# One key and one value piece per step in a cached attention's decode, TensorE's order written out there, and the start of the second group's decode moved

## The chip, the cores and the metric

The kernel runs on one core of one Trainium2 chip. A core has TensorE (PE, matmuls and transposes), VectorE (DVE), ScalarE (ACT), GpSimd (POOL) and SyncE (SP, which here only issues DMAs), each with its own queue of instructions. The time is that of one execution on the device in microseconds, lower is better; the median of several runs is given.

## What is computed

One layer of an encoder on a prompt of 1024 tokens and, beside it, on 8 sequences of 16 new tokens that have a cache of past keys and values. The heads fall in two groups of 8: group A does stick-breaking attention over the full past, group B attention over a band with a learned bias.

```
h = rmsnorm(x, g_mix)
q_a, k_a, v_a, q_b, k_b, v_b = split_heads(h, w_in)
# prompt:  a   = stick_breaking(q_a, k_a, v_a)          o_b = chunk_band_prompt(q_b, k_b, v_b, rel_table)
# decode:  a   = stick_breaking(q_a, [past_sb_k, k_a], [past_sb_v, v_a])      past of 1024
#          o_b = band_attention(q_b, [past_cb_k, k_b], [past_cb_v, v_b])      past of 512
x = x + concat(rmsnorm(a), rmsnorm(o_b)) @ w_out
h = rmsnorm(x, g_ffn)
x = x + (silu(h @ w_gate) * (h @ w_up)) @ w_down
x = x + sigmoid(rmsnorm(x, g_ple) @ w_ple_gate) * (p @ w_ple_proj)

def stick_breaking(q, k, v):
    z = einsum('bqhd,bkhd->bhqk', q, k) * HEAD_DIM ** -0.5
    log_keep = where(causal, log_sigmoid(-z), 0)
    between = cumsum(log_keep, reverse) - log_keep
    w = where(causal, exp(log_sigmoid(z) + between), 0)
    return einsum('bhqk,bkhd->bqhd', w, v)
```

The new keys and values are outputs too.

## The kernel before

Tokens are rows: 8 tiles of 128 prompt tokens and one tile of 128 decode tokens (8 sequences x 16), so 9 tiles or 3 token groups of 384. Every f32 operand of the projections is split in a high and a low part, and a product is three matmuls (`mm3`, L105 to L107); the low part of weights, `wlo`, is made by POOL, and the helper that makes it has one line, L110.

The part of the program that matters here has four stages. First the hidden state is normed and transposed into `hT` (two halves of the rows, three token groups, high and low). Then `project` (the generator `qkv`) runs over twelve chunks of 256 columns of `w_in`, (group, q/k/v, chunk); `queries` and `others` yield after each piece of about 24 matmuls. 36 of its yields run by themselves. In the next 30, A's decode runs beside it: `advance(project, dec, 2.2, 30)` calls the decode 2.2 times for each yield of the projection. Then A's attention (`att`) runs beside the rest of the projection, the last chunk of which is (1, 0, 1), B's second query chunk; after it the pools of the projection close. Last, B's decode and the product with `w_ple_proj` (`embed`, whose sums are named pj) run beside the rest of attention: six yields of the decode to one of attention's stages, then `along(dec, embed(), 0.55)` at 1.3 for each.

The decode works on sequences n (a batch, 16 tokens x 8 heads = 128 rows) and chunks c of 256 cached tokens; 4 chunks for A, 2 for B. Its list `seq` alternates a key piece and a value piece, the value pieces some places behind. `fetch` loads a piece of 512 KB into a buffer `draw` (7 buffers in A, 6 ahead; in B one less) over SP's queue, L134. `prepare` of a key piece makes eight transposes (L383) and copies them to `kT`; that of a value piece transposes two or three tiles of weights `wdec` and `wn` (L392, in `flip`). `scores` are four matmuls into rows of 32 of `sdec` (L406), and on the last chunk one with the causal mask (L409); `outputs` are four per tile of values, into `acc` (L449). A matmul of f32 leaves two records in the trace, a bf16 one. When a batch has all its scores, `weights` makes the scan over keys and the multiply on DVE (L424, L425) and `wn` on POOL (L437). A step of the decode handles one piece: fetch six ahead, prepare two ahead, then scores or outputs.

In attention S are the scores (L551), `w` the weights, whose last product is made by POOL (L566, tiles of 128x127 to 128x1023), then transposed on PE (L584) and split by ACT and DVE, and po are the outputs (L607, L608). In B's decode POOL also scales `bias` (L327) and adds the two parts of new values, queries and keys, `nv`, `sq`, `sk` (L341, L334).

The order on each engine comes from Tile's scheduler, which simulates a timeline of all engines and puts each engine's instructions in the order that it finds. A block under `tc.manual_schedule(engines={...})` keeps, on the engines named, the order in which the code issues. Buffers of a pool are laid over those of closed pools, and an instruction that writes one waits until the last reader of the old contents is done.

Of the kernel before, what the change touches and what calls it, by code (L numbers as in the profile page):

```python
# [22 lines left out]
P = 128  # L23
# [9 lines left out]
SKEW = 2  # L33
LAG, RAWS, PT = 5, 7, 2
# [4 lines left out]
def tile_hymba_step(  # L39
# [119 lines left out]
    class Transposed:  # L159
# [5 lines left out]
        def add(self, pool, half, name):  # L165
            for n in range(2):
                for g in range(3):
                    self.t[n][g][half] = pool.tile([P, KT // 2, 384], F32R, name=f"{name}{'hl'[n]}{g}{half}")
# [47 lines left out]
    def qkv(ch, hT, stg):  # L216
# [16 lines left out]
        def queries(grp, c, wts):  # L233
            wh, wl = wts
            for pr in range(2):
                m = slice(pr * P, (pr + 1) * P)
                for g in range(3):
                    ps_ = ps["o"].tile([P, 384], F32, name="ps", tag="O")
                    for k in range(KT):
                        mm3(ps_, wh[:, k, m], wl[:, k, m], *hT.rows(g, k), k == 0, k == KT - 1)  # L240
                    transposed_out(grp, 0, c * 2 + pr, g, parts(384, ps_, (1 - 2 * grp) * HD**-0.5))
                    yield

        def others(grp, w, c, wts, gs):

            wh, wl = wts
            for g in gs:
                st = stg.tile([P, 3, 256], F32, name="st", tag="st", bufs=2)
                for o in range(3):
                    ps_ = ps["o"].tile([P, 256], F32, name="ps", tag="O")  # L250
                    for k in range(KT):
                        mm3(ps_, *hT.tok(g * 3 + o, k), wh[:, k], wl[:, k], k == 0, k == KT - 1)
                    (V.tensor_copy if o % 2 else A.copy)(st[:, o], ps_)
                    if o < 2:
                        yield
# [29 lines left out]
                yield  # L285
# [28 lines left out]
    def decode(grp, ch, dk):  # L314

        odd = dk.tile([P, 2], F32, name="odd")
        nc.sync.dma_start(odd, consts[:, 0:2])
        nkc = (4, 2)[grp]
# [29 lines left out]

        ks = [("k", n, c) for n in range(8) for c in range(nkc)]
        vs = [None] * (nkc + VLAG[grp]) + [("v", n, c) for n in range(8) for c in range(nkc)]  # L350
        seq = [x for pieces in zip_longest(ks, vs) for x in pieces if x]
        raws, split = {}, {}

        def fetch(i):
            kind, n, c = seq[i]
            src = ((cache_sb_k, cache_cb_k) if kind == "k" else (cache_sb_v, cache_cb_v))[grp]
            src = src[0, n, c * 256 : (c + 1) * 256]
            raws[i] = ch.raw(src.rearrange("(n p) h d -> p n (h d)", p=P), 2, 512)
# [38 lines left out]
        def scores(st, c, kT):  # L397
# [9 lines left out]
            if grp == 0:  # L407
                if masked:
                    T.matmul(sc[:, 256:], lhsT=identb, rhs=causalb, start=False, stop=True)  # L409
# [317 lines left out]
    hT.add(hp, 0, "hT")  # L727
    hT.add(hp, 1, "hT")
# [18 lines left out]
    advance(project, dec, 2.2, 30)  # L747
    for _ in dec:
        pass
# [65 lines left out]
    advance(att, dec, 0, 6)  # L815
    beside = along(dec, embed(), 0.55)
    advance(att, beside, 1.3, 40)
# [658 lines left out]
```

## Time and profile before

| what | value |
|---|---|
| median of 3 runs | 1763.65 us (1763.17 to 1764.24) |
| the profiled execution | 1761.44 us |
| its span in the trace | 1759.7 us |
| mean granted TensorE clock | 0.985 |
| PE, DVE, POOL, ACT busy | 1688.2, 1051.2, 804.7, 761.6 us |
| share of PE in the chain that ended last | 86% |

In the trace of the profiled execution, A's decode lies between about 139 and 325 us, the rest of the projection, beside attention, to about 527, B's decode and `embed` from there to about 700. The page of the profile has one number of busy time for each engine; a window does the same for a stretch, with the granted clock (1.00 is full) and the share of time for which the DMA engines were busy. In a timeline each row is one instruction or a run of like ones (x8), with its start, its duration and in brackets the idle time of the engine before it and who ended it. The end of a matmul is modelled, so the pace is read from the starts.

### The profile page before, as it was taken

To read this page: it belongs to the slowest core of one execution; us is meant where nothing else is said; L and a number is where in the kernel's file an instruction comes from. 1 tells how busy PE (TensorE), PEld (TensorE's weight loads), DVE (VectorE), ACT (ScalarE), POOL (GpSimd) and SP (SyncE) were. 2 spreads that over 40 slices of the span, in tenths; PEclk is the share of its full clock that TensorE was granted. 3 is DMA by queue.
4 is the path that set the end of the run, shared out by engine and by line. 5 is a ranking of instruction groups with operands and counts; after the bars stand their busy time and mean duration, and the time that the engine had idled before them with its cause. 6 is when DMAs were issued, how large, how long until landed. Compare 5 with 4: busy or idle time off the path is not lost.

```text
span 1759.7 us, 29028 instructions
## 1 busy us (share of the span) xinstructions
PE 1688.2 (96%) x11048; PEld 1469.3 (84%) x11048; DVE 1051.2 (60%) x1638; ACT 761.6 (43%) x1646; POOL 804.7 (46%) x635
## 2 busy tenths in 40 slices
PE   7999999999996899899989999999999999999998
PEld 7998888889995687787868888888888788887998
DVE  5212444257778566653686666666666598878635
ACT  5213434367766567743553333333233333333532
POOL 3214321277559322312345555555555465558354
PEclk9999999999998899999999999999999999999999
DMA  6756887656468696855422222222222684411123
GB/s 210 252 187 201 292 270 267 187 159 171 137 173 232 199 264 196 222 169 187 163 83 90 93 93 93 93 93 92 95 93 93 235 327 138 138 51 60 48 80 138
DMA packets 183467, 279.93 MB, mean 159 GB/s; under 512 B 15264, under 2 KB 115232, under 8 KB 181920
## 3 DMA queue, kind: packets, MB, share of 16 engines
q1 hardware_dynamic: 183328, 278.07, 49.4%
q8 instruction: 88, 1.44, 0.3%
q14 instruction: 51, 0.42, 0.1%
HBM read 198.47 MB, written 79.56 MB: 158 GB/s over the span
## 4 chain that ended last, share of the span: by engine, by line
PE 86%; DMA 4%; DVE 4%; POOL 3%; ACT 2%; issue 1%; SPq 0%; POOLq 0%; ACTq 0%; DVEq 0%
PE ps L998 19%; PE ps L105 9%; PE ps L106 9%; PE ps L107 8%; PE pt L1249 6%; PE ps L1249 4%; PE pt L998 3%; PE pt L584 3%; PE pt L383 2%; PE acc L449 2%; PE po L608 2%; PE po L607 2%; PE S L551 2%; PE sdec L406 1%; DMA v<-sv 1%
## 5 line engine op out<-in xcount | busy, mean ns | idle before, releaser
L110 POOL TENSOR_TENSOR wlo<-wraw,whi 128x512 fp32r<-128x512 f32 (+1 forms) x128 | 232.7, 1846 | 233.1 <-ACT whi L149 228.8
L105 PE MATMUL ps<-whi,hTh 128*128 128x256 f32 x576 | 168.9, 293 | 1.0 <-ACT sq L222 0.6
L106 PE MATMUL ps<-wlo,hTh 128*128 128x256 f32 x576 | 165.9, 288 | 1.0 <-POOL wlo L110 1.0
L107 PE MATMUL ps<-whi,hTl 128*128 128x256 f32 x576 | 166.6, 289 | 0.0
L149 ACT CAST whi<-wraw 128x512 fp32r<-128x512 f32 (+1 forms) x132 | 90.4, 749 | 98.0 <-PE ps L998 65.7
L565 DVE TENSOR_TENSOR_SCAN keep<-keep,zero 128x128 f32<-128x128 f32 (+4 forms) x64 | 100.9, 1585 | 38.5 <-ACT keep L557 37.8
L566 POOL TENSOR_TENSOR w<-w,keep 128x127 f32<-128x127 f32 (+4 forms) x64 | 89.2, 1405 | 66.4 <-DVE keep L565 57.9
L105 PEld LDWEIGHTS ps<-whi,hTh 128*128 128x128 f32 x576 | 110.9, 193 | 7.2 <-issue 5.0
L110 DVE TENSOR_TENSOR wtl<-pt,wth 128x512 fp32r<-128x512 f32 (+1 forms) x192 | 94.7, 514 | 32.0 <-ACT wth L588 31.1
L106 PEld LDWEIGHTS ps<-wlo,hTh 128*128 128x128 f32 x576 | 110.9, 192 | 3.2 <-issue 1.8
L107 PEld LDWEIGHTS ps<-whi,hTl 128*128 128x128 f32 x576 | 111.0, 193 | 0.3 <-issue 0.2
L584 PE MATMUL pt<-ident,w 128*128 128x128 f32 x528 | 92.0, 286 | 17.2 <-POOL w L566 13.5
L588 ACT CAST wth<-pt 128x512 fp32r<-128x512 f32 (+1 forms) x192 | 84.4, 464 | 37.8 <-PE pt L584 37.4
L584 PEld LDWEIGHTS pt<-ident,w 128*128 128x128 f32 x528 | 64.4, 146 | 27.1 <-POOL w L566 14.3
L105 PE MATMUL ps<-whi,hVh 128*128 128x256 f32 x288 | 81.8, 284 | 0.5 <-ACT hVh L1396 0.5
L106 PE MATMUL ps<-wlo,hVh 128*128 128x256 f32 x288 | 81.7, 284 | 0.0
L607 PE MATMUL po<-wth,vk 128*128 128x256 f32 (+1 forms) x304 | 80.7, 294 | 1.0 <-DVE wtl L110 1.0
L107 PE MATMUL ps<-whi,hVl 128*128 128x256 f32 x288 | 81.5, 284 | 0.0
L551 PE MATMUL S<-qk 128*128 128x384 f32 (+2 forms) x192 | 73.5, 385 | 4.7 <-DVE mxp L560 1.7
L608 PE MATMUL po<-wtl,vk 128*128 128x256 f32 (+1 forms) x304 | 77.0, 294 | 0.0
L384 DVE COPY kT<-pt 128x512 f32<-128x512 f32 x48 | 32.9, 688 | 65.9 <-PE pt L383 59.7
L110 POOL TENSOR_TENSOR actl<-actr,acth 128x1024 fp32r<-128x1024 f32 (+1 forms) x22 | 56.5, 2571 | 33.9 <-DMA sr<-acts 18.2
(351 smaller groups left out, 5402.6 us busy)
## 6 DMA issues: line engine op xcount, KB each, us to landing
draw<-in_cache_sb_k SPq DMA_DIRECT2D x32, 512.0 KB
draw<-in_cache_sb_v SPq DMA_DIRECT2D x32, 512.0 KB
act<-sg SPq DMA_DIRECT2D x11, 1152.0 KB
actr<-act SPq DMA_DIRECT2D x22, 576.0 KB
wraw<-in_w_in SPq DMA_DIRECT2D x12, 1024.0 KB
wraw<-in_w_gate SPq DMA_DIRECT2D x11, 1024.0 KB
wraw<-in_w_up SPq DMA_DIRECT2D x11, 1024.0 KB
v<-sv SPq DMA_DIRECT2D x36, 256.0 KB
```

The costliest lines, as they stand in the source:

```text
L105: T.matmul(out, lhsT=ah, rhs=bh, start=start, stop=False)
L106: T.matmul(out, lhsT=ah, rhs=bl, start=False, stop=False)
L107: T.matmul(out, lhsT=al, rhs=bh, start=False, stop=stop)
L110: eng.tensor_tensor(out, a, hi.bitcast(F32), op=ALU.subtract)
L149: A.copy(h[:, o], v[:, o])
L551: T.matmul(sc, lhsT=hd["qq"][:, qs], rhs=hd["kkh"][:, kc], start=True, stop=False)
L565: V.tensor_tensor_scan(rev, rev, zero[:, 0:1].to_broadcast([P, n]), 1.0, op0=ALU.mult, op1=ALU.add)
L584: T.transpose(pt[:, (c - c0) * P : (c - c0 + 1) * P], w[:, c * P : (c + 1) * P], ident)
L607: T.matmul(dst, lhsT=vs, rhs=wth[:, kb - base, c0:c1], start=(i == 0), stop=False)
L608: T.matmul(dst, lhsT=vs, rhs=wtl[:, kb - base, c0:c1], start=False, stop=(i == nkb - 1))
L998: T.matmul(out, lhsT=a[x][:, k], rhs=b[y][:, k], start=(not more and k == 0 and n == 0), stop=(k == 3 and n == 2), skip_group_check=more)
L1249: T.matmul(out, lhsT=a[i][:, x, m * P : (m + 1) * P], rhs=b[j][:, x], start=(not more and x == 0 and n == 0), stop=(x == 1 and n == 2), sk ...
```

## The change

`hT` is allocated token group by token group. The last query chunk, (1, 1) in `queries`, runs by token groups: both pairs of heads of group 0, then of group 1, then of group 2. `others` yields after each tile of tokens. The decode issues its first loads ahead of its constants; a step handles a key piece and a value piece together, prepares the next step's pieces, makes the scores and outputs of its own, then weights and finish. A's decode advances 1.2 steps for each yield of the projection, and PE's order there is that of the code. The mask is four matmuls of 32 columns. B's decode is called three times at its start instead of six, then 1.0 to `embed` and 1.0 to attention.

```diff
--- before.py
+++ after.py
+R2 = 1.2
...
-        def add(self, pool, half, name):
-            for n in range(2):
-                for g in range(3):
+        def add(self, pool, half, name, gs=range(3)):
+            for g in gs:
+                for n in range(2):
...
         def queries(grp, c, wts):
             wh, wl = wts
-            for pr in range(2):
+            order = [(pr, g) for pr in range(2) for g in range(3)]
+            if (grp, c) == (1, 1):
+                order.sort(key=lambda x: x[1])
+            for pr, g in order:
                 m = slice(pr * P, (pr + 1) * P)
-                for g in range(3):
...
         def others(grp, w, c, wts, gs):
...
                     (V.tensor_copy if o % 2 else A.copy)(st[:, o], ps_)
-                    if o < 2:
-                        yield
+                    yield
...
-                yield
...
     def decode(grp, ch, dk):
+        nkc = (4, 2)[grp]
+        ks = [("k", n, c) for n in range(8) for c in range(nkc)]
+        vs = [None] * (nkc + VLAG[grp]) + [("v", n, c) for n in range(8) for c in range(nkc)]
+        seq = [x for pieces in zip_longest(ks, vs) for x in pieces if x]
...
+        ahead = ch.raws - 1
+        for i in range(ahead):
+            fetch(i)
         odd = dk.tile([P, 2], F32, name="odd")
         nc.sync.dma_start(odd, consts[:, 0:2])
...
                 if masked:
-                    T.matmul(sc[:, 256:], lhsT=identb, rhs=causalb, start=False, stop=True)
+                    for pr in range(4):
+                        o = slice(pr * 32, pr * 32 + 32)
+                        T.matmul(sc[o, 256:], lhsT=identb[:, o], rhs=causalb, start=False, stop=True)
...
-        ahead = ch.raws - 1
-        for i in range(ahead):
-            fetch(i)
+        steps, at = [], 0
+        for pieces in zip_longest(ks, vs):
+            n = sum(x is not None for x in pieces)
+            steps.append(range(at, at + n))
+            at += n
         yield
-        for i in range(AHEAD):
+        for i in steps[0]:
             prepare(i)
-        for i, (kind, n, c) in enumerate(seq):
-            if i + ahead < len(seq):
-                fetch(i + ahead)
-            if i + AHEAD < len(seq):
-                prepare(i + AHEAD)
-            x, wt = split.pop(i)
-            if kind == "k":
-                scores(batch[n], c, x)
+        for j, step in enumerate(steps):
+            for i in step:
+                if i + ahead < len(seq):
+                    fetch(i + ahead)
+            for i in steps[j + 1] if j + 1 < len(steps) else ():
+                prepare(i)
+            for i in step:
+                kind, n, c = seq[i]
+                (scores if kind == "k" else outputs)(batch[n], c, *split.pop(i))
+            for i in step:
+                kind, n, c = seq[i]
                 if c == nkc - 1:
-                    weights(batch[n])
-            else:
-                outputs(batch[n], c, x, wt)
-                if c == nkc - 1:
-                    finish(batch[n])
+                    (weights if kind == "k" else finish)(batch[n])
             yield
...
-    hT.add(hp, 0, "hT")
-    hT.add(hp, 1, "hT")
+    for g in range(3):
+        for half in range(2):
+            hT.add(hp, half, "hT", (g,))
...
-    advance(project, dec, 2.2, 30)
-    for _ in dec:
-        pass
+    with tc.manual_schedule(engines={mybir.EngineType.PE}):
+        advance(project, dec, R2, 30)
+        for _ in dec:
+            pass
...
     next(dec)
-    advance(att, dec, 0, 6)
-    beside = along(dec, embed(), 0.55)
-    advance(att, beside, 1.3, 40)
+    advance(att, dec, 0, 3)
+    beside = along(dec, embed(), 1.0)
+    advance(att, beside, 1.0, 40)
```

In the code after, lines stand one to twelve further down: L383 of before is L389, L392 is L398, L406 is L412, L409 is L417, L449 is L457, L566 is L576, and L105 to L107 are L106 to L108.

The program's order on PE in the middle of A's decode, before. The matmuls of the projection (ps) that fill the places marked are left out; draw are raw keys, pt a bank for transposes.

```order
L392 MATMUL pt<-ident,wdec 128x128 x2
L449 MATMUL acc<-draw,wt 32x128 x8
L406 MATMUL sdec<-kT,qbd_1609 32x256 x4
L392 MATMUL pt<-ident,wdec 128x128 x2
...
L449 MATMUL acc<-nv,wt 32x128 x4
L449 MATMUL acc<-draw,wt 32x128 x8
...
L383 MATMUL pt<-ident,draw 128x128 x4
...
L392 MATMUL pt<-ident,wdec 128x128 x2
L383 MATMUL pt<-ident,draw 128x128 x4
L449 MATMUL acc<-draw,wt 32x128 x8
```

The same engine after, in the same stretch: two steps, the first one with a batch's first weights, the second with the outputs of its new values.

```order
L389 MATMUL pt<-ident,draw 128x128 x8
L398 MATMUL pt<-ident,wn 128x128
L398 MATMUL pt<-ident,wdec 128x128 x2
L412 MATMUL sdec<-kT,qbd_1623 32x256 x4
L457 MATMUL acc<-draw,wt 32x128 x8
...
L389 MATMUL pt<-ident,draw 128x128 x8
L398 MATMUL pt<-ident,wdec 128x128 x2
L412 MATMUL sdec<-kT,qbd_1623 32x256 x4
L457 MATMUL acc<-nv,wt 32x128 x4
L457 MATMUL acc<-draw,wt 32x128 x8
```

Scores and outputs of a step now stand beside each other, and every step has the same form; before, outputs were split from scores, and the transposes of one key piece were cut in two.

POOL's order at the end of the projection and the start of B's decode, before.

```order
L345 MEMSET qbd_6680 128x128
L435 COPY wn<-zero 128x128 x2
L110 TENSOR_TENSOR wlo<-wraw,whi 128x1024 x2
L327 TENSOR_SCALAR bias<-bias 128x528
L341 TENSOR_TENSOR nv<-sv 128x512
L566 TENSOR_TENSOR w<-w,keep 128x767
L566 TENSOR_TENSOR w<-w,keep 128x895
L116 TENSOR_TENSOR r_o<-r_o,nhalf 128x16
L566 TENSOR_TENSOR w<-w,keep 128x1023
L566 TENSOR_TENSOR w<-w,keep 128x127
```

POOL there after.

```order
L443 COPY wn<-zero 128x128 x2
L111 TENSOR_TENSOR wlo<-wraw,whi 128x1024 x2
L576 TENSOR_TENSOR w<-w,keep 128x767
L576 TENSOR_TENSOR w<-w,keep 128x895
L117 TENSOR_TENSOR r_o<-r_o,nhalf 128x16
L576 TENSOR_TENSOR w<-w,keep 128x1023
L344 TENSOR_SCALAR bias<-bias 128x528
L576 TENSOR_TENSOR w<-w,keep 128x127
L655 TENSOR_TENSOR osb<-osb,r_o 128x8x64 x2
L358 TENSOR_TENSOR nv<-sv 128x512
```

The scaling of bias and the sum of new values have moved behind larger tiles of attention's weights; the weight split, `wlo`, has stayed ahead of them.

SP's queue some 20 us later, in B's decode, before; sk and sq are the new keys and queries of the decode, toep a table of attention's bias, vk the values of a head pair.

```order
L332 DMA sq_6667<-qT1l 128x4x128
L772 DMA pn<-in_p_prompt 128x256 x2
L648 DMA mixp_89<-osb 128x8x128
L519 DMA vk<-v_86 128x8x128
L332 DMA sk_6672<-kT1l 128x4x128
L134 DMA draw<-in_cache_cb_v 128x2x512
L134 DMA draw<-in_cache_cb_k 128x2x512
L527 DMA toep<-in_rel_table 128x640
```

And after.

```order
L349 DMA sq_6704<-qT1l 128x4x128
L784 DMA pn<-in_p_prompt 128x256 x2
L135 DMA draw<-in_cache_cb_v 128x2x512
L658 DMA mixp_89<-osb 128x8x128
L135 DMA draw<-in_cache_cb_k 128x2x512
L349 DMA sk_6709<-kT1l 128x4x128
L529 DMA vk<-v_86 128x8x128
L784 DMA pn<-in_p_prompt 128x256
```

The second load of new keys, from kT1l, has moved ahead of that of vk. Further up the same queue, the first cache loads of B stand ahead of the loads of constants and of the first part of new keys, behind which they stood.

## Rows read from the trace of the kernel before

**Rows 1.** the page, section 1: busy us, share of the span, instructions.

```profile
PE 1688.2 (96%) x11048; PEld 1469.3 (84%) x11048; DVE 1051.2 (60%) x1638; ACT 761.6 (43%) x1646; POOL 804.7 (46%) x635
```

**Rows 2.** waits of PE, whole span: us in total, times, longest us.

```profile
PE pt L584 <- POOL w L566: 13.5, 4, 6.4
```

**Rows 3.** windows: us, busy us by engine, PEclk, DMA share, GB/s.

```profile
160.00:340.00 180.00, 179.50 (x1956) 152.18 (x1957) 69.58 (x99) 75.67 (x198) 49.52 (x65) 1.00 0.77 252
...
525.00:585.00 60.00, 39.59 (x267) 33.88 (x265) 40.48 (x51) 34.39 (x79) 48.47 (x35) 0.85 0.81 231
```

**Rows 4.** timeline of PE, among A's decode: start us, us, instruction.

```profile
182.13 0.28 PE L106 MATMUL ps<-wlo,hTh 128*128 128x256 f32 x1
182.25 0.28 PE L107 MATMUL ps<-whi,hTl 128*128 128x256 f32 x1
182.46 0.67 PE L406 MATMUL sdec<-kT,qbd 128*32 128x272 f32 x8
183.06 0.18 PE L409 MATMUL sdec<-causalb,identb 128*128 128x16 bf16 x1
183.09 1.07 PE L383 MATMUL pt<-ident,draw 128*128 128x128 f32 x8
...
184.31 0.65 PE L449 MATMUL acc<-draw,wt 128*32 128x128 f32 x16
184.89 0.39 PE L105 MATMUL ps<-whi,hTh 128*128 128x256 f32 x1
185.11 0.28 PE L106 MATMUL ps<-wlo,hTh 128*128 128x256 f32 x1
```

**Rows 5.** timeline of PE, a block with the new values' outputs.

```profile
196.15 0.64 PE L406 MATMUL sdec<-kT,qbd 128*32 128x256 f32 x8
196.61 0.40 PE L449 MATMUL acc<-nv,wt 128*32 128x128 f32 x8
196.82 0.62 PE L449 MATMUL acc<-draw,wt 128*32 128x128 f32 x16
197.38 0.38 PE L106 MATMUL ps<-wlo,hTh 128*128 128x256 f32 x1
```

**Rows 6.** instructions of PE by line, 160 to 340: busy, mean ns | idle.

```profile
L383 PE MATMUL pt<-ident,draw 128*128 128x128 f32 x222 | 31.7, 276 | 0.0
```

**Rows 7.** timelines of DVE, POOL and PE behind the mask matmul at 183.06.

```profile
188.62 3.23 DVE L425 TENSOR_TENSOR wdec<-wdec,keep 128x1039 f32<-128x1039 f32 x1
...
204.37 1.24 DVE L425 TENSOR_TENSOR wdec<-wdec,keep 128x1039 f32<-128x1039 f32 x1
...
184.02 6.74 POOL L110 TENSOR_TENSOR wlo<-wraw,whi 128x1024 fp32r<-128x1024 f32 x2 [0.27 <-POOL qbd L374]
...
193.03 0.33 PE L392 MATMUL pt<-ident,wn 128*128 128x128 f32 x1
```

**Rows 8.** waits on SP's queue, 140 to 340.

```profile
SPq L134 <- POOL wlo L110: 7.5, 3, 5.3
```

**Rows 9.** timeline of PE: waits for POOL's w, in brackets the idle time.

```profile
373.74 0.47 PE L584 MATMUL pt<-ident,w 128*128 128x128 f32 x1 [3.19 <-POOL w L566]
...
541.62 1.54 PE L584 MATMUL pt<-ident,w 128*128 128x128 f32 x6 [6.43 <-POOL w L566]
```

**Rows 10.** timeline of POOL ahead of these two waits.

```profile
361.57 6.23 POOL L110 TENSOR_TENSOR wlo<-wraw,whi 128x1024 fp32r<-128x1024 f32 x2 [0.92 <-ACT whi L149]
...
527.39 6.17 POOL L110 TENSOR_TENSOR wlo<-wraw,whi 128x1024 fp32r<-128x1024 f32 x2
533.53 3.24 POOL L327 TENSOR_SCALAR bias<-bias 128x528 f32<-128x528 f32 x1
...
537.96 5.33 POOL L566 TENSOR_TENSOR w<-w,keep 128x767 f32<-128x767 f32 x2
...
562.97 1.29 POOL L334 TENSOR_TENSOR sk<-sk,sk 128x512 f32<-128x512 f32 x1 [3.30 <-DMA sk<-kT1l]
```

**Rows 11.** the page, section 6: DMA issues, count, KB each.

```profile
draw<-in_cache_sb_k SPq DMA_DIRECT2D x32, 512.0 KB
```

More of the change, by code (lines that the diff above doesn't have):

```diff
@@ L234, in queries @@
             wh, wl = wts
-            for pr in range(2):
+            order = [(pr, g) for pr in range(2) for g in range(3)]
+            if (grp, c) == (1, 1):
+                order.sort(key=lambda x: x[1])
+            for pr, g in order:
                 m = slice(pr * P, (pr + 1) * P)
-                for g in range(3):
[L238 to L241, printed above, removed]
-                    yield
+                ps_ = ps["o"].tile([P, 384], F32, name="ps", tag="O")
+                for k in range(KT):
+                    mm3(ps_, wh[:, k, m], wl[:, k, m], *hT.rows(g, k), k == 0, k == KT - 1)
+                transposed_out(grp, 0, c * 2 + pr, g, parts(384, ps_, (1 - 2 * grp) * HD**-0.5))
+                yield
         def others(grp, w, c, wts, gs):
@@ L253, in others @@
                     (V.tensor_copy if o % 2 else A.copy)(st[:, o], ps_)
-                    if o < 2:
-                        yield
+                    yield
                 if w == 1:
@@ L284, in others @@
                     )
-                yield
         loads = [(0, 1, 0), (0, 1, 1), (0, 0, 0), (0, 0, 1), (0, 2, 0), (0, 2, 1),
@@ L314, in decode, with fetch @@
     def decode(grp, ch, dk):
+        nkc = (4, 2)[grp]
+        ks = [("k", n, c) for n in range(8) for c in range(nkc)]
+        vs = [None] * (nkc + VLAG[grp]) + [("v", n, c) for n in range(8) for c in range(nkc)]
+        seq = [x for pieces in zip_longest(ks, vs) for x in pieces if x]
+        raws, split = {}, {}
+        def fetch(i):
+            kind, n, c = seq[i]
+            src = ((cache_sb_k, cache_cb_k) if kind == "k" else (cache_sb_v, cache_cb_v))[grp]
+            src = src[0, n, c * 256 : (c + 1) * 256]
+            raws[i] = ch.raw(src.rearrange("(n p) h d -> p n (h d)", p=P), 2, 512)
+        ahead = ch.raws - 1
+        for i in range(ahead):
+            fetch(i)
         odd = dk.tile([P, 2], F32, name="odd")
         nc.sync.dma_start(odd, consts[:, 0:2])
-        nkc = (4, 2)[grp]
         if grp == 0:
@@ L347, in decode @@
         batch = [{"b": b} for b in range(8)]
[L349 to L358, printed above, removed]
         def prepare(i):
@@ L395, in flip, with scores @@
             return wt
-        def scores(st, c, kT):
+        def scores(st, c, kT, _):
             last = c == nkc - 1
@@ L467, in finish @@
             nc.sync.dma_start(mixs[grp][b * 16 : b * 16 + 16, :].rearrange("i (h d) -> h i d", h=8), ow)
-        ahead = ch.raws - 1
-        for i in range(ahead):
-            fetch(i)
+        steps, at = [], 0
[3 more added lines that the diff above has]
+            at += n
         yield
-        for i in range(AHEAD):
+        for i in steps[0]:
             prepare(i)
-        for i, (kind, n, c) in enumerate(seq):
-            if i + ahead < len(seq):
-                fetch(i + ahead)
-            if i + AHEAD < len(seq):
-                prepare(i + AHEAD)
-            x, wt = split.pop(i)
-            if kind == "k":
-                scores(batch[n], c, x)
-                if c == nkc - 1:
-                    weights(batch[n])
-            else:
-                outputs(batch[n], c, x, wt)
-                if c == nkc - 1:
-                    finish(batch[n])
+        for j, step in enumerate(steps):
[8 more added lines that the diff above has]
+            for i in step:
+                kind, n, c = seq[i]
+                if c == nkc - 1:
+                    (weights if kind == "k" else finish)(batch[n])
             yield
```

## The prediction

> **What bounds the kernel now.** I read the page first: TensorE (PE) is busy 1688.2 us, 96% of the span [rows 1]. So nothing that other engines save counts unless PE waits for them, and there are two ways to gain: make PE's own stream shorter, or remove one of its few waits. The page's list of what PE waited for leads with the transposes of attention's weights, L584, behind GpSimd (POOL), 13.5 us in four waits [rows 2]. Then I cut the changed part into stretches. From 160 to 340 us, A's decode among the projection, PE is busy 179.50 of 180.00 us at full clock: only a shorter stream helps there. From 525 to 585 us, the end of the projection and the start of B's decode, PE is busy 39.59 of 60.00 us, at 0.85 of the clock, and POOL 48.47: POOL sets the pace [rows 3]. Last I read single instructions to get unit prices.
>
> **The price of an excursion.** The decode's scores (L406) and outputs (L449) run on 32-column tiles (128\*32 in the rows), everything else on 128\*128. In a plain stretch a projection matmul starts 0.12 us after the last (182.13, 182.25). From there to the first score it is 0.21, so 0.09 for entering. From the sixteen output records at 184.31 to the next L105 at 184.89 it is 0.58 us; a block with eight records more takes 0.77, from 196.61 to 197.38 [rows 4, 5]. Eight records cost 0.19, sixteen 0.39; 0.19 of the 0.58 is the price of leaving. The second matmul behind, at 185.11, is 0.22 after the first instead of 0.12: 0.10 more. Together 0.38 us per excursion. Cross-check: scores followed by a 128-wide matmul take 0.60 us (182.46 to 183.06), followed by outputs 0.46 (196.15 to 196.61) [rows 4, 5]; the difference of 0.14 is the leaving again, and staying among 32-column tiles is free of it.
>
> **Part 1: one key and one value piece in one step, PE's order fixed.** In the orders, A's decode has 60 excursions before and 37 after; matmul counts are the same but for the mask. 23 x 0.38 = **+8.7 us**. As PE has no idle time in that stretch, this lies on the path. Bounds: 23 x 0.14 = 3.2 (the leaving alone) to 23 x 0.48 = 11 (were entry 0.1 dearer, as the 0.09 is one reading).
>
> **Part 2: the mask in four 32-column matmuls.** 24 more in all. Behind the one 128-wide L409 the next matmul starts 0.03 us later [rows 4], so 24 x 0.03 = 0.7 us; at the price of scores in a block, 0.46 us for four [rows 5], 24 x 0.115 = 2.8. Taken: **-0.7**, the row of the same 16-column shape. In the new order the mask stands between scores and outputs. The Trainium skill, TensorEngine Tiling (Array Packing), Key Properties under Tiling Modes, says that changing the tiling mode, not just the tile, drains TensorE. By it a 128-wide mask there would add an excursion in each of eight batches, 3.0 us, and the narrow form saves these; by the 0.03 us behind L409 alone, which stood at the end of its block, the wide form would have cost nothing. The sum holds neither: it counts the excursions as they stand in the orders.
>
> **Part 3: new PE waits under the fixed order.** Before, the scheduler placed each decode matmul where its simulated operands were ready; now scores, weights' transposes and outputs stand as the code yields them. Transposes of raw tiles never waited before (0.0 us idle at L383 [rows 6]). The danger is the first value step of each of the eight batches: mask matmul, sigmoid, scan, multiply, copy, then PE's transpose of the weights. In one batch this took from 183.06 (mask matmul) to 193.03 (transpose), 9.97 us [rows 4, 7]; the multiply L425 took 3.23 us beside POOL's weight split, and 1.24 when alone [rows 7]. Behind the mask matmul the new order leaves, by my unit prices, 5.5, 9.4, 9.4, 7.0, 10, 10, 6.4 and 7.4 us of other PE work. Were the chain 9.97 each time, the shortfalls add up to 4.5+0.6+0.6+3.0+0+0+3.6+2.6 = 14.9 us. With the multiply alone, 1.99 less, the chain is 8.0 and the sum 2.5+0+0+1.0+0+0+1.6+0.6 = 5.7; in the quiet batches other waits fall away too. I take **-3**, below the second end, because the scan's wait is shorter where ACT is free, with 0 to -14.9 as bounds. What queues behind a waiting transpose on PE is the whole projection.
> The Trainium skill, GPSIMD Engine Reference, in its Key points, says that GpSimd shares its SBUF interfaces with VectorE and contends with two-input instructions. It speaks against the change: L425 has two inputs, and the trace agrees where the split runs (3.23 us against 1.24). By it the long chain is limited to batches beside a split, about three of eight, some 4 us in all.
>
> **Part 4: cache loads.** A step issues both its loads at its head, on SP's queue. The look-ahead stays six pieces. Today the longest that SP waits there with a load for a buffer is 5.3 us [rows 8]. The cover is two steps of PE work; a step is 24 x 0.12 + 1.22 (L383 and L392, 183.09 to 184.31) + 0.60 + 0.58 = 5.3 us [rows 4], two 10.6. I cost it at nothing; the second rival is what it costs if that cover is gone.
>
> **Part 5: from 345 to 380 us.** PE stops 3.19 us at L584 for POOL's multiply w [rows 9]. POOL does that multiply behind a 6.23 us weight split (361.57) [rows 10]; in the order after, the multiply of 767 comes ahead of the split. **+3** (the wait), from -2 (the split now is late for the projection) to +6 (the slow clock behind the wait too).
>
> **Part 6: B's decode.** PE waits 6.43 us at 541.62 for w [rows 9]. POOL reaches w of 767 at 537.96, behind the split at 527.39 and two instructions of decode set-up, bias and new values, begun at 533.53 [rows 10]. These two now stand later, and w of 767 starts 537.96-533.53 = 4.4 us earlier. On SP the second load of new keys moves ahead of one of values; POOL idled 3.30 us for it at 562.97 [rows 10]. The first raw transposes move up in front of attention's, which puts about 4 us of PE work under the stretch that POOL bounds. The 3.3 and the 4 may well end in the wait for the next POOL result, so I count the **+4.4** alone, with 1 to 12 as bounds. The first raw loads stand ahead of the constants' and new keys' on SP and are laid over token group 0, which the last query chunk now finishes first; that costs the bias nothing, since POOL takes it later. The first wait of attention's S in A may grow, as less decode work stands behind the last query chunk: **-0.5** (-3 to +1). B's decode has 36 excursions instead of 42: 6 x 0.38 = **+2.3**.
>
> **The sum.** 8.7 - 0.7 - 3 + 3 + 4.4 - 0.5 + 2.3 = 14.2 us. The profiled execution took 1761.44 us, so 1747.2 there; the median of the runs is 2.2 higher: **1749.4 us**.
>
> **Rivals.** *The fixed order stalls at every weights' transpose.* 14.9 instead of 3: 11.9 us more, 1761.3 us. For it: all eight chains as long as the one in rows 7. Against: a split runs beside a few. *Cache loads come late (slower side).* Steps issue loads in pairs. A piece is 512 KB [rows 11]; four in flight at 252 GB/s [rows 3] take 4 x 524 KB / 252 GB/s = 8.3 us. If once per batch SP is held for 5.3 us, its wait for a weight split [rows 8], then 5.3 + 8.3 - 10.6 = 3.0 us of PE waiting, 24 us in eight batches: 1749.4 + 24 = 1773.4. It decides from a landing time over 5.3 us behind the longest hold. Against: that hold comes where the weights of a new chunk load, three times, and L383 has no wait today [rows 6]. *Only the excursions are saved*, the POOL-bound stretches give nothing, PE waits elsewhere for the same results: 8.7 + 2.3 - 0.7 - 3 = 7.3 us, 1756.4.
>
> **How the numbers follow.** Changes within 0.2%, 3.5 us, can't be told from none. Chances: forecast 0.5; excursions alone 0.25 (both faster); stalls at the transposes 0.13 (most of it within 0.2%: 0.09, the rest a little faster or slower); late loads 0.12, of which 0.1 slower. So faster 0.78, same 0.1, slower 0.12. Range: below, the upper bounds of parts 5 and 6 (3 + 7.6) and no wait in part 3 (3) together are unlikely, and two thirds of their sum, 9, gives 1740; above, it takes in the stalls, 1763.
>
> **What would show it.** In A's decode, PE's timeline has one block of L406 and L449 neighbours per step, and the stretch ends some 6 to 9 us sooner with idle times at the weights' transposes (L392 of before) of a microsecond or two; over 10 us in all there, rival one. Idle time at raw transposes (L383) says rival two. The 6.43 us wait at the end of the projection shrinks to about 2; if it reappears behind the next w, the third rival. The gap in B before the first scores stays where the load of toep ends it. Wrong it would be if excursions cost less when blocks are longer, or if the scheduler's places on other engines shift their work behind PE's.

## The result and the profile after

The changed kernel takes 1742.53 us, median of four runs (1739.81 to 1744.19), beside 1763.41 us for the kernel before on the same chip: a ratio of 0.988, interval 0.9863 to 0.9897, 20.9 us faster. The forecast was 1749.4 us, the range 1740 to 1763. Run again in a later set, the same kernel took 1739.84 us beside 1764.6, 0.9866 (0.9845 to 0.9888). So two variants less than 3 us apart are not told apart here.

The profiled execution of the changed kernel took 1742.95 us, with a span of 1741.2 us, 18.5 less than before. Its page, PE against [rows 1]:

```profile
span 1741.2 us, 29075 instructions
...
PE 1675.4 (96%) x11072; PEld 1468.0 (84%) x11072; DVE 1043.8 (60%) x1638; ACT 764.6 (44%) x1646; POOL 803.3 (46%) x635
```

The share is the same 96%: PE became shorter, 1688.2 to 1675.4 us, and its idle time went down with it. Three marks in PE's timelines, each the start of one instruction, say where the 18.5 us lie.

| mark on PE | before | after | gained so far |
|---|---|---|---|
| first score S of A's attention | 342.83 | 335.86 | 7.0 |
| last matmul of the projection | 524.65 | 516.18 | 8.5 |
| first transpose of the FFN's rows | 854.42 | 835.74 | 18.7 |

The rest of the kernel, behind the last mark, is 905 us long and takes 0.2 us more. So A's decode brought 7.0, the projection beside attention 1.5, and B's decode with what stands beside it 10.2.

A step of A's decode in PE's timeline after (start, duration, line, shapes), to be laid beside [rows 4, 5]:

```profile
193.92 0.38 PE L398 MATMUL pt<-ident,wdec 128*128 128x128 f32 x2
194.23 0.64 PE L412 MATMUL sdec<-kT,qbd 128*32 128x256 f32 x8
194.69 0.62 PE L457 MATMUL acc<-draw,wt 128*32 128x128 f32 x16
195.24 0.39 PE L106 MATMUL ps<-whi,hTh 128*128 128x256 f32 x1
195.46 0.28 PE L107 MATMUL ps<-wlo,hTh 128*128 128x256 f32 x1
```

Scores go straight into outputs after 0.46 us, and the leaving is paid once, behind the outputs.

What PE waited for between 139 and 340 us, after (total, times, longest):

```profile
PE pt L389 <- ACT kT L390: 0.7, 2, 0.5
PE pt L389 <- DVE kT L390: 0.6, 1, 0.6
PE pt L389 <- DVE sq L111: 0.3, 1, 0.3
PE S L562 <- DMA qk<-kT0l: 0.2, 1, 0.2
```

There is no wait at L398, the weights' transpose, and none for a raw load.

### The profile page after: what moved, and what is told of

Read it like the earlier page. It is cut to its first block, busy times and chain, and to the rows that moved or that the text cites. A ratio compares the mean times of both kernels' runs of the same rounds, so it can differ in the third digit from the quotient of the medians.

```text
span 1741.2 us, 29075 instructions
## 1 busy us (share of the span) xinstructions
PE 1675.4 (96%) x11072; PEld 1468.0 (84%) x11072; DVE 1043.8 (60%) x1638; ACT 764.6 (44%) x1646; POOL 803.3 (46%) x635
## 4 chain that ended last, share of the span: by engine, by line
PE 87%; DMA 5%; DVE 2%; ACT 2%; POOL 2%; issue 1%; SPq 1%; POOLq 0%; ACTq 0%; DVEq 0%
PE ps L1010 20%; PE ps L106 9%; PE ps L107 9%; PE ps L108 9%; PE pt L1261 6%; PE ps L1261 4%; PE pt L1010 3%; PE pt L594 3%; PE pt L389 2%; PE po L618 2%; PE S L561 2%; PE po L617 2%; PE acc L457 2%; PE sdec L412 1%; PE S L562 1%
## 5 line engine op out<-in xcount | busy, mean ns | idle before, releaser
L111 POOL TENSOR_TENSOR wlo<-wraw,whi 128x512 fp32r<-128x512 f32 (+1 forms) x128 | 228.9, 1816 | 216.1 <-ACT whi L150 214.5
L106 PE MATMUL ps<-whi,hTh 128*128 128x256 f32 x576 | 168.7, 293 | 0.7 <-ACT sq L223 0.6
L107 PE MATMUL ps<-wlo,hTh 128*128 128x256 f32 x576 | 165.9, 288 | 1.0 <-POOL wlo L111 1.0
L108 PE MATMUL ps<-whi,hTl 128*128 128x256 f32 x576 | 166.1, 288 | 0.0
L106 PEld LDWEIGHTS ps<-whi,hTh 128*128 128x128 f32 x576 | 111.9, 194 | 6.6 <-issue 5.4
L576 POOL TENSOR_TENSOR w<-w,keep 128x127 f32<-128x127 f32 (+4 forms) x64 | 89.4, 1408 | 52.6 <-DVE keep L575 47.9
L107 PEld LDWEIGHTS ps<-wlo,hTh 128*128 128x128 f32 x576 | 111.8, 194 | 1.4 <-POOL wlo L111 1.3
L108 PEld LDWEIGHTS ps<-whi,hTl 128*128 128x128 f32 x576 | 111.7, 194 | 0.2 <-issue 0.2
L106 PE MATMUL ps<-whi,hVh 128*128 128x256 f32 x288 | 82.0, 285 | 0.5 <-ACT hVh L1408 0.5
L107 PE MATMUL ps<-wlo,hVh 128*128 128x256 f32 x288 | 81.6, 283 | 0.0
L108 PE MATMUL ps<-whi,hVl 128*128 128x256 f32 x288 | 81.6, 284 | 0.0
L106 PE MATMUL ps<-hTh,whi 128*128 128x384 f32 x192 | 65.9, 343 | 0.0
```

The costliest lines, as they stand in the source:

```text
L106: T.matmul(out, lhsT=ah, rhs=bh, start=start, stop=False)
L107: T.matmul(out, lhsT=ah, rhs=bl, start=False, stop=False)
L108: T.matmul(out, lhsT=al, rhs=bh, start=False, stop=stop)
L111: eng.tensor_tensor(out, a, hi.bitcast(F32), op=ALU.subtract)
```

## The experiments

The net time below is PE's time from the same matmul of the projection in each kernel (the one at about 49 us behind a wait of 0.61 us for ACT) to the first S, less the idle time in the rows between. It still holds what a lower clock costs. In all these kernels but one the granted clock is full in this stretch. An excursion, as before, is a stay of PE in 32-column tiles.

**Scores and outputs apart.** The step's transposes stand between them; everything else is as in the changed kernel.

```diff
+            if grp == 1:
+                for i in steps[j + 1] if j + 1 < len(steps) else ():
+                    prepare(i)
+            for i in step:
+                kind, n, c = seq[i]
+                if kind == "k":
+                    scores(batch[n], c, *split.pop(i))
+            if grp == 0:
+                for i in steps[j + 1] if j + 1 < len(steps) else ():
+                    prepare(i)
...
-                (scores if kind == "k" else outputs)(batch[n], c, *split.pop(i))
+                if kind == "v":
+                    outputs(batch[n], c, *split.pop(i))
```

> The changed kernel with scores and outputs of each step of A's decode set apart again: the next step's transposes now stand between them. Same matmuls, same loads, same fixed order; 59 excursions instead of 37. By the excursions, 22 x 0.38 = 8.4 us: about 1751, first S near 344. Rival, that the gain came from the shorter queue of other engines' work or from the uniform order: within 1.5 us of the changed kernel.

Measured: 1761.19 us, 0.9987 of before (0.9976 to 0.9998). PE's timeline of it, one step and two waits:

```profile
194.59 0.64 PE L412 MATMUL sdec<-kT,qbd 128*32 128x256 f32 x8
195.16 1.09 PE L389 MATMUL pt<-ident,draw 128*128 128x128 f32 x8
196.09 0.38 PE L398 MATMUL pt<-ident,wdec 128*128 128x128 f32 x2
196.41 0.65 PE L457 MATMUL acc<-draw,wt 128*32 128x128 f32 x16
196.98 0.39 PE L106 MATMUL ps<-whi,hTh 128*128 128x256 f32 x1
...
178.65 0.64 PE L412 MATMUL sdec<-kT,qbd 128*32 128x256 f32 x8 [2.10 <-ACT kT L390]
...
279.74 0.55 PE L263 MATMUL pt<-ident,st 128*128 128x128 f32 x3 [2.54 <-DVE kT L390]
```

The first S comes at 351.50, 15.6 us later than in the changed kernel: twice the expectation. The net time is 292.73 against 284.54 us, 8.19 us more for 22 excursions. Not all of it is their price: behind the wait of 2.54 us TensorE ran for 3.4 us, from 280.6, at half its clock (1.2 GHz for 2.4). The view of two of these us, and three projection matmuls there, which start 0.21 us apart instead of 0.12:

```profile
281.00:283.00 2.00, 2.00 (x12) 2.00 (x11) 0.77 (x2) 0.00 (x0) 0.19 (x1) 0.50 1.05 344
...
280.61 0.41 PE L107 MATMUL ps<-wlo,hTh 128*128 128x256 f32 x1
280.81 0.41 PE L108 MATMUL ps<-whi,hTl 128*128 128x256 f32 x1
281.02 0.41 PE L106 MATMUL ps<-whi,hTh 128*128 128x256 f32 x1
```

Sixteen such matmuls, from 280.61 to 284.01, cost 1.5 us more than at full clock. That leaves 6.7 us for the excursions, 0.30 each. The other half of the delay is idle time, 9.97 against 1.58 us: the transposes of raw keys now stand behind the scores, so their copies to kT stand behind the work on those scores in the queues of ACT and DVE, and PE waits for the copies, as the two bracketed rows show. Ahead of the second one, DVE makes the scan first and the copy behind it:

```profile
275.73 3.37 DVE L432 TENSOR_TENSOR_SCAN keep<-keep,zero 128x1040 f32<-128x1040 f32 x1 [2.61 <-ACT keep L419]
279.03 0.66 DVE L390 COPY kT<-pt 128x512 f32<-128x512 f32 x1
```

That wait was in nobody's expectation. It belongs to the place of the transposes, not to the excursions, and it would have spoiled the reading of the whole time alone.

**PE's order free.** The block of fixed order is taken away.

```diff
-    with tc.manual_schedule(engines={mybir.EngineType.PE}):
-        advance(project, dec, R2, 30)
+    advance(project, dec, R2, 30)
```

> The changed kernel without the fixed order of TensorE in A's decode: the scheduler places the same steps itself. It has 49 excursions into 32-column tiles there instead of 37 (60 before the change). If the gain up to the first score of A's attention (342.8 to 335.9 us, 7.0) comes from excursions at 0.38 us each, 12 more cost 4.6 us: about 1747 us, first S near 340. Rival, that the fixed order costs waits which the scheduler avoids: the same or 1 to 3 us faster than the changed kernel, with fewer waits at raw transposes (2 us there now).

Measured: 1744.51 us, 0.9897 (0.9882 to 0.9912). Net time 288.16 us, 3.62 more for 12 excursions, 0.30 each, the same price as above; idle time 0.16 instead of 1.58. So the fixed order buys 3.6 us of shorter stream for 1.4 us of waits: counted from that matmul, the first S is 2.2 us later without it. In the whole time the two can't be told apart. The expectation and its rival were each right about their own half.

**The mask as one matmul.**

```diff
-                    for pr in range(4):
-                        o = slice(pr * 32, pr * 32 + 32)
-                        T.matmul(sc[o, 256:], lhsT=identb[:, o], rhs=causalb, start=False, stop=True)
+                    T.matmul(sc[:, 256:], lhsT=identb, rhs=causalb, start=False, stop=True)
```

> The changed kernel with the mask as one 128-wide matmul. It then stands between scores and outputs, and the decode of A has 44 excursions instead of 37. By the price of an excursion 7 x 0.37 = 2.6 us lost, less some 1 us for 24 matmuls left out: first S 1.6 us later, net of idle time. Rival, that a matmul of 16 columns costs what the row behind it says (0.03 us) and no change of mode: 0.7 us sooner. The whole time is expected within 2 us of the changed kernel, so the net time up to the first S decides.

Measured: net time 286.33 us, 1.79 more, where 1.6 was expected. With 0.30 us for each of 7 excursions, 2.1, the 24 matmuls left out were worth 0.3 us, 0.013 each. The rival falls: the wide form is dearer amid a block although the next matmul came 0.03 us behind L409 at the end of one. The whole time is 1739.33 us, 0.9865 (0.985 to 0.9879), not to be told from the changed kernel's two medians: B's stage came out shorter in this kernel, by a schedule that differs there too.

**Only A's decode changed.** hT, the last query chunk, the place of B's first loads, B's single pieces and their pace are as before.

> Only the changes in A's decode (pairs, fixed order, mask in four); hT, the last query chunk, the place of B's first loads, B's steps and their pace as before. By the excursions the first score of A's attention stands near 336 as in the changed kernel, and what is gained behind the projection is gone: 7 to 9 us faster than before, about 1755. Rival, that the parts behind the projection gain nothing by themselves: as fast as the changed kernel, 1743.

Measured: 1756.09 us, 0.9958 (0.9943 to 0.9973). The first S is at 334.83, net 284.57 us as in the changed kernel. So A's part alone is worth 6.5 us by the medians and 7.4 by the ratio, and what was gained behind the projection is gone. The rival falls.

**Token groups, first loads.** The first of these allocates hT and runs the last query chunk as before; the second issues B's first six loads behind the constants.

```diff
-            if (grp, c) == (1, 1):
-                order.sort(key=lambda x: x[1])
```

> The changed kernel with hT allocated and the last query chunk run as before (pair by pair, not by token group). If the 10 us that the changed kernel gains behind the end of the projection come from B's raw tiles being loaded sooner, the first raw transpose in B goes back by some 10 us against the projection's end and most of 5 us are lost: about 1747. Rival, that the pace of decode against attention does it: within 1.5 us of the changed kernel.

Measured: 1739.9 us, 0.9868 (0.9854 to 0.9883). B's first raw transpose is at 537.32, not later than in the changed kernel (542.07, and 538.76 in its second run); behind the last matmul of the projection it comes 23.62 us later, and 25.89 and 23.62 there. The token groups are worth nothing that can be measured, and the expectation falls.

```diff
         ahead = ch.raws - 1
-        for i in range(ahead):
-            fetch(i)
+        if grp == 0:
+            for i in range(ahead):
+                fetch(i)
...
+        if grp == 1:
+            for i in range(ahead):
+                fetch(i)
```

> The changed kernel with B's first six cache loads issued behind the constants and new keys again, as before. On POOL the scaling of bias and the sum of new values then stand ahead of attention's weights of 767 again. If that order is what shortened PE's wait there from 6.43 to 3.30 us, the wait is back at about 6.4 us and 3 to 5 us are lost: about 1747. Rival, that POOL-bound time only moves: within 1.5 us of the changed kernel, another wait for w shorter by as much.

Measured: 1741.45 us, 0.9876 (0.9858 to 0.9895). POOL's order is that of before at this place, and so is PE's wait. PE's waits for POOL in the timeline, of this kernel and then of the changed one:

```profile
531.82 1.54 PE L598 MATMUL pt<-ident,w 128*128 128x128 f32 x6 [6.43 <-POOL w L580]
...
552.57 0.64 PE L413 MATMUL sdec<-kT,qbd 128*32 128x256 f32 x8 [1.15 <-POOL qbd L381]
```

```profile
528.36 1.54 PE L594 MATMUL pt<-ident,w 128*128 128x128 f32 x6 [3.30 <-POOL w L576]
...
536.97 1.97 PE L594 MATMUL pt<-ident,w 128*128 128x128 f32 x8 [0.63 <-POOL w L576]
...
545.06 0.44 PE L594 MATMUL pt<-ident,w 128*128 128x128 f32 x2 [0.76 <-POOL w L576]
551.75 0.68 PE L412 MATMUL sdec<-kT,qbd 128*32 128x256 f32 x8 [2.14 <-POOL qbd L380]
```

The 6.43 us are back, and the whole time shows no loss by it: the waits shown add up to 7.6 us in this kernel and to 6.8 in the changed one, where bias and the new values stand later on POOL and PE waits for POOL behind 536. The rival was right: in this stretch, which POOL bounds, reordering POOL's work moved PE's wait. From the last matmul of the projection to the FFN this kernel's profiled execution takes 322.1 us, the changed kernel's two 319.6 and 319.2, so a loss of up to 3 us can't be excluded.

**Pairs, start and pace in B.** The calls first, since the first of them is told wrongly ahead of the prediction and in the expectations:

```python
    def advance(main, side, ratio, steps=None):

        due, n = 0.0, 0
        while steps is None or n < steps:
            if next(main, "end") == "end":
                break
            n += 1
            due += ratio
            while due >= 1.0:
                due -= 1.0
                next(side, None)
        return n
```

`advance(att, dec, 0, 6)` advances attention, its first argument, by six stages and calls the decode 0 times for each. So the six and the three are not calls of the decode: the changed kernel starts B's decode behind three stages of attention, where the kernel before ran six. Behind that start, the kernel before gives the decode 1.3 / (1 + 0.55) = 0.84 pieces for each stage of attention, and the changed kernel 1.0 / (1 + 1.0) = half a pair, which is one piece.

Four kernels, with the A part as changed. In the first, B's decode is in pairs but is called as the old code called it, so at 1.7 pieces for each stage; in the second, it is in single pieces at the old calls; in the third, in single pieces at 6, 0.5, 1.5, one piece for each stage; in the fourth, in pairs at 3, 1.1, 0.88, so 0.84 pieces.

```diff
-    advance(att, dec, 0, 3)
-    beside = along(dec, embed(), 1.0)
-    advance(att, beside, 1.0, 40)
+    advance(att, dec, 0, 6)
+    beside = along(dec, embed(), 0.55)
+    advance(att, beside, 1.3, 40)
```

The single pieces are the old loop, for B alone:

```diff
+        if grp == 1:
+            for i in range(AHEAD):
+                prepare(i)
+            for i, (kind, n, c) in enumerate(seq):
...
+                if i + AHEAD < len(seq):
+                    prepare(i + AHEAD)
+                (scores if kind == "k" else outputs)(batch[n], c, *split.pop(i))
...
+                yield
+            return
```

> The changed kernel with B's decode and the embedding product called at the old pace (six steps of decode at the start, 0.55 and 1.3 for each stage). If the pace carries the gain behind the projection, 3 to 6 us are lost: 1746 to 1749. Rival, that the sooner loads do it: within 1.5 us of the changed kernel. Since a step is now two pieces, six calls at the start put twice the old work ahead of attention, so a loss could also be that.

> The changed kernel with B's decode in single pieces at the old pace (six calls at the start, 0.55, 1.3); A's decode, loads first and the last query chunk as changed. B has 42 excursions instead of 36: by their price of 0.37 us, 2.2 us are lost, about 1745. Rival, that the pairs and their pace carry most of the 10 us gained behind the projection, for B's decode ends sooner and PE has less idle time: 1750 or more.

> The changed kernel with B's decode in single pieces, called at the changed kernel's pace counted in pieces: six at the start, 0.5 of the embedding product to a piece, 1.5 for each stage of attention. Before it was 0.84 pieces a stage, now it is one. If the pace carries the gain behind the projection (more of the decode's PE work laid under the stretch that POOL bounds), most of the 12 us lost with pieces at the old pace come back: 1743 to 1747, with 52 us or more of full-clock PE work in the first 75 us behind the projection. Rival, that the pairs as such do it: about 1755, 48 us.

> The changed kernel with pairs in B's decode, but the old pace counted in pieces: 1.1 of the embedding product to a pair, 0.88 for each stage of attention (0.84 pieces a stage). If the pace carries the gain: 5 to 10 us lost, 1748 to 1752. Rival, that the pairs do it: within 2 us of the changed kernel.

The third column is the start of B's first raw transpose behind the last matmul of the projection, the fourth the way from that matmul to the first transpose of the FFN's rows, both in the profiled execution.

| B's decode | stages ahead, embed, pace | first raw transpose | to the FFN | median, us | interval of the ratio |
|---|---|---|---|---|---|
| pairs | 6, 0.55, 1.3 | 35.95 | 331.3 | 1754.38 | 0.9937 to 0.9969 |
| single pieces | 6, 0.55, 1.3 | 35.80 | 330.0 | 1756.42 | 0.9955 to 0.9983 |
| single pieces | 6, 0.5, 1.5 | 35.86 | 323.5 | 1746.78 | 0.9885 to 0.992 |
| pairs | 3, 1.1, 0.88 | 32.74 | 319.1 | 1741.73 | 0.9857 to 0.9899 |
| pairs (the changed kernel) | 3, 1.0, 1.0 | 25.89, 23.62 | 319.6, 319.2 | 1742.53, 1739.84 | 0.9863 to 0.9897, 0.9845 to 0.9888 |

The first 75 us behind the last matmul of the projection, as windows (stretch, length, busy time of PE, PEld, DVE, ACT, POOL, then PE's granted clock, DMA share, GB/s): before; pairs at the old calls; pieces at the old calls; pieces at 1.5; pairs at 0.88; the changed kernel; and the kernel with late loads from above.

```profile
524.65:599.65 75.00, 53.93 (x393) 44.74 (x392) 49.43 (x81) 43.57 (x103) 50.96 (x46) 0.84 0.71 203
```

```profile
515.82:590.82 75.00, 50.80 (x385) 41.96 (x384) 49.60 (x79) 42.91 (x102) 48.31 (x46) 0.89 0.70 199
```

```profile
514.37:589.37 75.00, 54.41 (x397) 45.09 (x396) 51.05 (x83) 44.68 (x106) 48.72 (x46) 0.89 0.72 203
```

```profile
514.01:589.01 75.00, 54.60 (x407) 43.90 (x405) 51.79 (x84) 44.72 (x106) 48.36 (x46) 0.93 0.73 210
```

```profile
514.43:589.43 75.00, 57.44 (x439) 48.00 (x438) 55.35 (x99) 49.35 (x117) 56.03 (x50) 0.93 0.77 227
```

```profile
516.18:591.18 75.00, 59.92 (x436) 50.56 (x434) 53.73 (x91) 47.47 (x113) 51.96 (x48) 0.89 0.77 230
```

```profile
514.84:589.84 75.00, 56.91 (x413) 48.15 (x412) 52.72 (x85) 45.10 (x107) 48.62 (x46) 0.86 0.76 225
```

Busy time times clock is the PE work at full clock that was got done there: 45.3 before, then 45.2, 48.4, 50.8, 53.4, 53.3 and 48.9 us. The changed kernel gets 8.0 us more decode and embedding work done there than the kernel before, while POOL holds attention. The reading is that this is what B's side of the change brought: work laid there, ahead of the stretches that PE bounds, is work that the end does not wait for. As a measure it is rough. The pieces at the old calls get 3.2 us more done than the pairs and are no faster, and the kernel with late loads, at 48.9, is as fast as the changed one. PE's idle time and slow clock over the whole way to the FFN follow the fourth column better: 46.7 us before, then 47.1, 44.3, 39.5, 35.5 and 38.7 in the rows of the table, 40.4 with late loads.

Of the expectations, that of the single pieces at the old pace falls and its rival holds, 1750 or more. Pace alone, from the second row to the third, brought 9.6 of the 14 to 17 us between the second row and the last, within the time that was expected, though with 50.8 us of work where 52 or more was to show it. But the fourth row keeps the old pace and loses nothing, against its expectation of 5 to 10 us. So a faster pace is enough for most of the gain, and it is not needed for it. The pairs at the old calls lost it all again, more than the 3 to 6 us expected: decode begins late there, and one wait of its scores for DVE (mxp) is 8.3 us instead of 4.0. The reason given with that expectation, twice the old work ahead of attention, is wrong, since the six are stages of attention.

One thing stays open. The run at 0.88 differs from the one in single pieces at the same pace in two things, the pairs and the start of the decode three stages of attention sooner. Which of them it is was not tried. The third column speaks for the start: the three kernels with six stages have their first raw transposes as late as the kernel before (36.05), whether in pairs or pieces.

**A faster pace.** Pairs at 3, 1.0, 1.2, with hT and the last query chunk as before; and the changed kernel beside it.

> The changed kernel with hT and the last query chunk as before and a pace of 1.2 for each stage of attention instead of 1.0. If more decode work under the POOL-bound stretch is what pays: some 3 to 5 us faster than the changed kernel, about 1738. Rival, that the decode, done sooner, leaves attention and the output projection alone later, with more waits for mixed rows (8.6 us there now): 1742 or more.

> The changed kernel itself, beside the three others of this set: 1742.5 us within 2 us.

Measured: 1738.38 us, 0.9853 (0.9837 to 0.9869), and 1739.84. The embedding product ends at 677.6 instead of 691.0 us, PE's work in the first 75 us goes up by some 2 us more, and the time goes down by 1.5, which is not clear of noise. The kernel with the old token groups above, which differs from this one in the pace alone, has 1739.9. The rival, 1742 or more, falls. Where the rest of what was expected went is not shown: the rival's place for it, the waits for mixed rows at the output projection, still leads PE's waits between 520 and 850 us (total, times, longest), but at 7.8 us, where the changed kernel's two runs have 8.6 and 8.9.

```profile
PE pt L853 <- DMA mixn<-mixp: 7.8, 4, 3.8
PE pt L592 <- POOL w L574: 7.5, 3, 3.3
PE sdec L410 <- DVE mxp L568: 1.7, 1, 1.7
```

## Why the prediction was right, and where not

**The number.** The profiled executions differ by 18.5 us, and 14.2 were forecast. Up to the first S it is 7.0 where 8.7 - 0.7 - 3 = 5.0 were added up; between there and the projection's end 1.5 for 3; behind it 10.2 for 4.4 + 2.3 = 6.7; the term of -0.5 is shown by no run. The time lies within the range, near its lower end, and that is in part luck: in A's decode two errors partly cancel, a gain priced too high and waits that did not come, and the term that was counted in B is not the one that paid.

**The bound.** Right. PE stayed at 96%, and each us of gain was a us of PE's stream, of its waits or of its slow clock. [rows 1, 3]

**The price of an excursion.** The mechanism is right and the size a quarter too high: 0.38 us from [rows 4, 5] against 0.30 in both runs that changed the number of excursions. Of the three parts of the 0.38, 0.09 for entering, 0.19 for leaving and 0.10 for the second matmul behind, the last is no price of the excursion. In the kernel before, the second projection matmul is as late behind plain 128-wide transposes:

```profile
195.01 0.38 PE L392 MATMUL pt<-ident,wdec 128*128 128x128 f32 x2
195.14 0.37 PE L105 MATMUL ps<-whi,hTh 128*128 128x256 f32 x1
195.35 0.28 PE L106 MATMUL ps<-wlo,hTh 128*128 128x256 f32 x1
```

Without it the rows give 0.28. Then 23 excursions fewer at 0.30, less 0.3 for the mask, are 6.6 us, for 8.0 forecast; the net time fell by 6.9 (291.46 to 284.54). With 1.0 less idle time that makes 7.9, of which the first S shows 7.0, because the stretch itself begins 1.0 us later (49.74 for 48.78). The wide mask lost 1.79 us, where the row behind L409 alone had it cost nothing. The Trainium skill, TensorEngine Tiling (Array Packing), Key Properties under Tiling Modes, says that a change of tiling mode drains TensorE; that run agrees with it.

**New PE waits, -3.** Not there. Idle time in that stretch fell from 2.59 to 1.58 us: new waits of 1.6 us in all stand at raw transposes, none at the weights' transposes, while one wait of scores (1.48) and one of the first S for its load (1.11) are gone. The step that failed is the chain behind the mask. It was priced from one batch in which POOL's weight split and the multiply ran at once [rows 7], and even in the kernel before that batch was the only one of its kind. DVE's multiplies (ns: shortest, median, longest; first and last start), before and after:

```profile
L425 DVE TENSOR_TENSOR wdec<-wdec,keep x8: 1232/1241/3230, 172.4 to 313.7; 128x1039 f32<-128x1039 f32 x8
```

```profile
L433 DVE TENSOR_TENSOR wdec<-wdec,keep x8: 1227/1241/1242, 175.0 to 310.4; 128x1039 f32<-128x1039 f32 x8
```

Seven of the eight took 1.23 or 1.24 us before, and all eight do now. The chain's last link ahead of the transpose is POOL's copy of the new weights. It ended 9.54 us behind the mask in the batch of [rows 7], 4.9 to 8.1 in the seven others, and after the change 4.9 to 6.6, where PE has 6.7 to 10.8 us of other work. One batch after, mask, copy and transpose:

```profile
189.49 0.19 PE L417 MATMUL sdec<-causalb,identb 128*32 128x16 bf16 x4
194.28 0.20 POOL L445 COPY wn<-wdec 128x16 f32<-128x16 f32 x1 [3.65 <-DVE wdec L433]
199.08 0.27 PE L398 MATMUL pt<-ident,wn 128*128 128x128 f32 x1
```

So the first rival had nothing to stand on. The second rival, late cache loads, did not come either: there is no wait of a raw transpose for a DMA up to 340 us.

**345 to 380 us, +3.** Half right. The 3.19 us wait [rows 9] is gone, but the projection ends only 1.5 us further ahead than the first S (2.3 in the second run of the changed kernel). PE met a new wait on ACT there:

```profile
350.31 0.50 PE L561 MATMUL S<-qk 128*128 128x512 f32 x1 [2.52 <-ACT keep L567]
```

**B's decode, +4.4 and +2.3.** Here the sum was mis-sized, 6.7 for 10.2, and for a wrong reason. The wait at the projection's end fell from 6.43 to 3.30 us, where about 2 was forecast, but undoing exactly that lost no time clear of noise: the term I counted is worth at most some 3 us, and what I named beside it and left out, work laid under POOL's stretch, goes with most of the 10.2, as the kernels with other calls of the decode show. The calls themselves were misread: the three and the six are stages of attention ahead of the decode. Of the 10.2 us, PE's idle time gives 4.3 (32.9 to 28.6 in the brackets from the projection's end to the FFN), its slow stretches 3.8 (granted clock below full, times busy time, in 5 us windows: 13.8 to 10.0), and net work at full clock 2.2 (283.1 to 280.9). The six excursions, 2.3 forecast and 1.8 at 0.30, may be that last part; it is not shown, for the pairs at the old calls have as few and 284.2 us of net work.

**The third rival**, only the excursions saved, falls with the 10.2 us behind the projection. Its half of the truth is the wait that only moved.

## What to carry to other kernels

Where one engine is busy all the time, read the price of its mode changes from the starts in a timeline, compare each start with the same start where no change stands, and count the changes in the order; here 0.30 us for each pair of changes came out of two experiments. Look at the granted clock before a longer stream is put down to the order. Where another engine bounds a stretch, don't count the wait that its reordering shortens; count how much of the bound engine's later work can be laid into that stretch. A chain should be priced from all its instances and not from the one contested one. And of a helper such as `advance`, read which of its arguments it steps.

## What the runs showed of the hardware that was not expected

The price of a 128-wide matmul amid 32-column tiles does not show in its own row: the next matmul started 0.03 us behind L409, and yet one such matmul set between scores and outputs made the net time 1.79 us longer in seven excursions, after 0.3 us saved.

Beside POOL's weight split, one 128x1039 multiply of DVE took 3.23 us [rows 7], and 1.23 or 1.24 in the fifteen other cases of the two kernels.
